# A Griffin-style layer in split fp32 on one core: the loads of the start untied from each other, and more units of the K loop done by Strassen products

## The chip, the core and the metric

The kernel runs on one core of one Trainium2 chip. A core has TensorE (PE, matrix products into PSUM), VectorE (DVE) and ScalarE (ACT) for elementwise work, GpSimd (POOL) for a few small operations and for issuing some transfers, and SyncE (SP), which here only issues transfers. Each engine takes its own instructions in order and waits on semaphores. The metric is the device time of one execution in microseconds.

## The reference

One layer on a residual stream x of 512 tokens by 2048 channels, all in float32 (cut; `GELU`, norms and attention are as they read):

```python
h = rmsnorm(x, attn_norm_g);  proj = h @ w_in                  # 2048 x 9216
u, v_sgu, q, k, v_att, g_a, g_b = split(proj)
y_a = chunked_spatial_gating(gelu(u), rmsnorm(gelu(v_sgu)), w_s, b_s)
y_b = stick_breaking_attention(rmsnorm(q), rmsnorm(k), v_att)
merged = sigmoid(g_a) * (y_a @ w_up_a) + sigmoid(g_b) * (y_b @ w_up_b)
x = x + merged @ w_o                                            # 2048 x 2048
hid = rmsnorm(x) @ w_ffn_in                                     # 2048 x 11264
x = x + (silu(gate) * up) @ w_ffn_out                           # 5632 x 2048
x = x + sigmoid(rmsnorm(x) @ w_ple_gate) * (p @ w_ple)
```

## The kernel before, in words

Everything is kept transposed, channels on the 128 partitions and the 512 tokens along the free axis. A float32 product is made of three matmuls: each operand is split into a high part (ACT copies it to fp32r: `whi` for weights, `parts` for activations) and a low part (DVE subtracts: `wlo`), and `mm3` adds hi*hi, hi*lo and lo*hi into PSUM (lines 268, 269 and 270).

The work is cut into **units**: 256 input channels by 256 output channels by 512 tokens. A *P* unit does the four 128x128 blocks plainly: 12 matmuls, 512 wide. An *S* unit does them as a Strassen form with seven products of blocks with 256 columns: 21 matmuls, 256 wide. Its activations need seven operand blocks (`Form`: the four blocks and three sums, all split), its weights too (`Weights`: two transfers from SP and one accumulating transfer from POOL into the same landing, two DVE sums, two ACT and two DVE splits). `Pair` works through all units of one output tile (256 channels); S units collect in banks that DVE and ACT mix at the end (line 673), P units add straight into y and z. Strings such as `OUT = "SSSSPPPP"` say which units of the K loop of a product are S and which P. The first output tile of every such product is done plainly. In w_in and w_ffn_in all units are S, for the most part in a doubled form (line 659, mixed at lines 702 and 705).

The stages follow each other: the first three products (`w_first`, eight K steps k with three P units each, while the x tiles are loaded, scaled, summed for the norm and split), the rest of w_in with attention and gating woven in, w_up_a/w_up_b, w_o, five small products of `w_ple`, w_ffn_in (44 tiles), w_ffn_out in three passes over K, and the gate w_ple_gate. Between stages the operand forms of the next product are made ahead, as room in two SBUF arenas (`parts` for split forms, `wholes` for raw blocks) comes free: `builds` is their queue, `tick` is called once or twice a unit and takes the next piece of such work.

Order: a scheduler that orders instructions by need sets each engine's order, except where extra edges hold it. `in_turn` keeps the weight splits and mixes in program order. `in_order` ties three kinds of loads on SP to one another: the first transfer of each weight block, and the x loads. `load_x` is called two steps ahead (`min(k + 3, KU)`).

A late S form (`late_form`, `plain_first`) makes its four sums (line 512, DVE) and then splits (lines 263 on ACT, 264 on DVE), when its turn in `builds` comes. `Norm.steps` (lines 907 to 933) sums squares over partitions with small matmuls (L914), makes diagonal matrices on DVE (L888) and multiplies them with ones on PE (L930), one piece a tick.

## Time and profile before

| | us |
|---|---|
| median of 3 runs | 2719.37 (2715.48 to 2728.74) |
| the profiled execution | 2723.71 |
| its span, first to last instruction | 2721.8 |
| PE busy | 2670.8 (98%) |
| DVE busy | 2166.5 (80%) |
| ACT busy | 1357.0 (50%) |
| POOL busy | 392.8 (14%) |

A busy PE is not a PE at its peak: matmuls overlap, so what a matmul costs is the distance from its start to the next one's start. The mean granted TensorE clock is 0.995. The stages stand at about 0 to 110 us (start), 110 to 860 (w_in), 860 to 1024 (w_up), 1024 to 1190 (w_o), 1190 to 1215 (w_ple), 1215 to 2064 (w_ffn_in), 2064 to 2246, 2246 to 2410 and 2410 to 2547 (the three passes of w_ffn_out) and from there the gate.

### The profile page before, as it was taken

Reading aid. Unit: us, or ns where it says so; the run is one execution under the profiler, and the core shown is the slowest. Engines: PE = TensorE matmul, PEld = TensorE weight load, DVE = VectorE, ACT = ScalarE, POOL = GpSimd, SP = SyncE. Lnnn points to the kernel's source line nnn. Section 1 sums busy time; section 2 is a strip of 40 time slices with the busy share of each in tenths; the row PEclk is TensorE's granted clock in tenths of the full one; section 3 lists DMA queues with packets and bytes.
Section 4 is the critical chain, followed back from the end, with each engine's and each line's share of the span. In section 5 each row is a group of like instructions: output and inputs, shape, how many; then the busy total and the mean of one; then the engine's idle time right before and its main releaser. Section 6 shows DMA issues by size and latency. Waiting matters only on the chain.

```text
span 2721.8 us, 43177 instructions
## 1 busy us (share of the span) xinstructions
PE 2670.8 (98%) x15907; PEld 2358.2 (87%) x15907; DVE 2166.5 (80%) x3715; ACT 1357.0 (50%) x2143; POOL 392.8 (14%) x439
## 2 busy tenths in 40 slices
PE   6999999999999999999999999999999999999999
PEld 5888888888888889988888888888888998989898
DVE  6687878788888657678989898989899567688876
ACT  6565656564555334365444444444445344454543
POOL 0112121211220000001111111111110111101110
PEclk8999999999999999999999999999999999999999
DMA  5667677777776447667888888788886668788784
GB/s 175 165 169 181 177 178 178 175 182 193 175 182 220 135 137 223 196 200 188 209 221 201 208 197 207 200 204 202 203 203 194 171 175 247 203 250 233 253 223 135
DMA packets 303412, 528.88 MB, mean 194 GB/s; under 512 B 25696, under 2 KB 162912, under 8 KB 303200
## 3 DMA queue, kind: packets, MB, share of 16 engines
q1 hardware_dynamic: 242448, 425.70, 49.1%
q0 software_dynamic: 60752, 100.43, 23.1%
q8 instruction: 125, 2.05, 0.3%
q14 instruction: 87, 0.71, 0.1%
HBM read 478.84 MB, written 47.19 MB: 193 GB/s over the span
## 4 chain that ended last, share of the span: by engine, by line
PE 84%; DVE 6%; DMA 4%; ACT 3%; issue 2%; POOL 0%; SPq 0%; DVEq 0%; ACTq 0%; POOLq 0%
PE ps L659 38%; PE ps L268 13%; PE ps L270 13%; PE ps L269 13%; PE small L659 4%; DVE wlo L344 2%; ACT whi L347 1%; DMA wholes<-w_in 1%; DVE parts L264 1%; DVE wholes L512 1%; DVE out L705 1%; DVE wholes L705 1%; PE small L1090 1%; PE small L1048 1%; DVE wholes L363 1%
## 5 line engine op out<-in xcount | busy, mean ns | idle before, releaser
L347 ACT ACTIVATE whi<-wholes 128x512 fp32r<-128x512 f32 (+4 forms) x950 | 846.9, 916 | 845.2 <-DVE wholes L363 286.4
L659 PE MATMUL ps<-parts,whi 128*128 128x512 f32 x3384 | 1127.1, 397 | 3.0 <-DVE p L705 1.9
L344 DVE TENSOR_TENSOR wlo<-wholes,whi 128x512 fp32r<-128x512 f32 (+4 forms) x950 | 961.6, 1044 | 97.5 <-ACT whi L347 96.5
L268 PE MATMUL ps<-parts,whi 128*128 128x256 f32 (+1 forms) x2675 | 857.3, 323 | 28.6 <-ACT whi L347 23.1
L269 PE MATMUL ps<-parts,whi 128*128 128x256 f32 (+1 forms) x2640 | 856.3, 324 | 0.9 <-DVE parts L264 0.9
L270 PE MATMUL ps<-parts,wlo 128*128 128x256 f32 (+1 forms) x2640 | 854.9, 324 | 1.8 <-DVE wlo L344 1.8
L659 PEld LDWEIGHTS ps<-parts,wlo 128*128 128x128 f32 x3384 | 634.9, 188 | 141.0
L659 PE MATMUL ps<-parts,wlo 128*128 128x256 f32 x3384 | 667.5, 278 | 0.0
L268 PEld LDWEIGHTS ps<-parts,whi 128*128 128x128 f32 x2675 | 509.5, 191 | 75.0 <-ACT whi L347 25.2
L659 PEld LDWEIGHTS ps<-parts,whi 128*128 128x128 f32 x3384 | 542.7, 189 | 10.2 <-issue 3.9
L269 PEld LDWEIGHTS ps<-parts,whi 128*128 128x128 f32 x2640 | 502.9, 191 | 45.1 <-DVE parts L264 2.2
L270 PEld LDWEIGHTS ps<-parts,wlo 128*128 128x128 f32 x2640 | 502.8, 190 | 41.0 <-DVE wlo L344 2.4
L363 DVE TENSOR_TENSOR wholes<-wholes 128x256 f32<-128x256 f32 (+1 forms) x794 | 327.7, 413 | 21.1 <-DMA wholes<-w_ffn_out 3.0
L351 POOL DMA_DIRECT2D wholes<-w_ffn_in x172 | 149.7, 870 | 752.4 <-DVE wlo L344 219.2
L705 DVE TENSOR_TENSOR out<-out,ps 128x256 f32<-128x256 f32 x373 | 152.9, 420 | 127.4 <-ACT out L702 116.6
L351 POOL DMA_DIRECT2D wholes<-w_in x132 | 116.7, 884 | 637.9 <-DMA wholes<-w_in 294.2
L264 DVE TENSOR_TENSOR parts<-wholes,parts 128x1024 fp32r<-128x1024 f32 (+3 forms) x129 | 122.4, 962 | 19.1 <-ACT parts L263 18.9
L659 PE MATMUL small<-parts,whi 128*128 128x512 f32 x344 | 136.0, 395 | 0.0
L1359 ACT ACTIVATE out<-out 128x512 f32<-128x512 f32 x44 | 27.8, 632 | 195.2 <-DVE out L1358 195.2
L263 ACT ACTIVATE parts<-wholes 128x1024 fp32r<-128x1024 f32 (+3 forms) x129 | 105.8, 844 | 32.7 <-DMA wholes<-hid 11.1
L351 POOL DMA_DIRECT2D wholes<-w_ffn_out x56 | 56.9, 1015 | 397.9 <-DMA wholes<-w_ffn_out 146.4
L673 DVE TENSOR_TENSOR out<-out 128x256 f32<-128x256 f32 x36 | 15.3, 424 | 120.5 <-ACT out L670 120.5
(125 smaller groups left out, 1655.2 us busy)
## 6 DMA issues: line engine op xcount, KB each, us to landing
wholes<-w_ffn_in SPq DMA_DIRECT2D x172, 384.0 KB, 5.5
wholes<-w_in SPq DMA_DIRECT2D x132, 384.0 KB, 5.1
wholes<-w_ffn_in SPq DMA_DIRECT2D x172, 256.0 KB, 4.7
wholes<-w_ffn_in POOLq DMA_DIRECT2D x172, 256.0 KB, 5.2
wholes<-w_in SPq DMA_DIRECT2D x132, 256.0 KB, 4.1
wholes<-w_in POOLq DMA_DIRECT2D x132, 256.0 KB, 4.9
wholes<-x SPq DMA_DIRECT2D x32, 512.0 KB, 5.4
wholes<-w_ffn_out SPq DMA_DIRECT2D x31, 512.0 KB, 4.2
```

The lines of the kernel that those rows point to most:

```text
L263: return (nc.scalar.activation(hi, src, AF.Copy), nc.vector.tensor_tensor(out=lo, in0=src, in1=hi.bitcast(F32), op=ALU.subtract))
L264: nc.vector.tensor_tensor(out=lo, in0=src, in1=hi.bitcast(F32), op=ALU.subtract))
L268: nc.tensor.matmul(ps[:, s], sh, mh[:, s], start=start, stop=False)
L269: nc.tensor.matmul(ps, sh, ml, start=False, stop=False)
L270: return nc.tensor.matmul(ps, sl, mh, start=False, stop=stop)
L344: in_turn(nc.vector.tensor_tensor(out=self.lo[:, blocks], in0=r, in1=h.bitcast(F32), op=ALU.subtract))
L347: in_turn(nc.scalar.activation(h, r, AF.Copy))
L351: nc.gpsimd.dma_start(out=raw[:, 3:5], in_=self.src[:, 1:3], accum_op=ALU.add)
L363: in_turn(nc.vector.tensor_tensor(out=o, in0=x, in1=y, op=ALU.add))
L659: i = nc.tensor.matmul(out, w, t, start=first and k == 0, stop=last and k == 1)
L705: in_turn(nc.vector.tensor_tensor(out=out, in0=x, in1=y, op=op))
L1359: nc.scalar.activation(g, g, AF.Silu)
```

## The change

Units: w_o has six S of eight in place of four, the first pass and the gate six of eight in place of five, the second pass six of seven in place of five. Since the first tile of the second product on is plain, that turns 16 + 7 + 7 + 7 = 37 P units into S units, one of them in the last tile of the gate. The last two S forms of w_o are made in the late form, with sums of their own.

Loads: `in_order` is gone, x loads are called when their step begins and take the block that was freed longest ago, p is loaded and split in halves, the first three results of w_ple are stored through POOL's queue, and five matmuls on zeros stand ahead of everything (`WARM`). In w_o the residual x is loaded three ticks into a tile, not a tile ahead, and the last tile is added to x before the second w_ple product, not after it.

Sums: `sum_early` scales a late form and makes its sums ahead of its turn, ten ticks after its fetch (`LANDS`), for the first three forms of the queue where room is. The norm's second matmul comes two ticks later.

The core of the diff:

```diff
-OUT = "SSSSPPPP"
-PASSES = "SSSSSPPP", "SSSSSPP", "SSSPPPP"
-GATE = "SSSSSPPP"
+OUT = "SSSSSSPP"
+PASSES = "SSSSSSPP", "SSSSSSP", "SSSPPPP"
+GATE = "SSSSSSPP"
+SUMMED = 4
+WARM = 5
+LANDS = 10
 def tick():
             if f.fetches and f.early and f.ready():
-                if fits([(wholes, f.fetches, "low"), (wholes, 1024, "low")]):
+                if fits([(wholes, f.fetches, "low")] + spare_blocks()):
                     f.fetch()
                 break
+        any(f.sum_early() for f in list(builds)[:FETCHED])
 class Weights:
             if kind == "P":
-                in_order(nc.sync.dma_start(out=raw, in_=src))
+                nc.sync.dma_start(out=raw, in_=src)
             else:
-                in_order(nc.sync.dma_start(out=raw[:, 3:5],
-                                           in_=src[:, 0:1].to_broadcast([P, 2, n * P])))
+                nc.sync.dma_start(out=raw[:, 3:5],
+                                  in_=src[:, 0:1].to_broadcast([P, 2, n * P]))
 class Form(Staged):
+        def sum_early(self):
+            if not self.late or self.sums or self.since is None or clock[0] < self.since + LANDS:
+                return False
+            if self.gain:
+                self.scale()
+            elif fits(SUMS + spare_blocks()):
+                self.sums = sums_of(self.raw)
+            return True
 def ple_operands():
-        raw = load(pT)
+        raw = take(1024)
         hi, lo = parts.take(1024, "high"), parts.take(1024, "high")
-        split_into(hi.own(), lo.own(), raw.f())
+        for s in (slice(0, T), slice(T, 2 * T)):
+            nc.sync.dma_start(out=raw.f()[:, s], in_=pT[:, s])
+            split_into(hi.own()[:, s], lo.own()[:, s], raw.f()[:, s])
 def ple_pair(j, planned=True):
-        nc.sync.dma_start(out=d, in_=o)
+        (nc.sync if planned else nc.gpsimd).dma_start(out=d, in_=o)
 def load_x():
-        x_raw.append(take(1024))
-        in_order(nc.sync.dma_start(out=x_raw[-1].f(), in_=xT[len(x_raw) - 1]))
+        x_raw.append(take(1024, "rested" if len(x_raw) < KU - 4 else "low"))
+        nc.sync.dma_start(out=x_raw[-1].f(), in_=xT[len(x_raw) - 1])
+    idle, nothing = wide(), bank()
+    nc.vector.memset(idle[:, : T // 2], 0.0)
+    for _ in range(WARM):
+        nc.tensor.matmul(nothing[:, :T // 2], idle[:, :P], idle[:, :T // 2],
+                         start=True, stop=True)
     ple_operands()
 class Norm: def steps
             diags = diagonals(self.cols)
             yield
+            yield
+            yield
 def x_form(k):
-            while len(x_raw) < min(k + 3, KU):
+            while len(x_raw) < min(k + 1, KU):
                 load_x()
+    def merged_form(j, kind):
+        src, ready = lambda: merged[j], lambda: j in merged
+        if kind == "S" and j >= SUMMED:
+            f = late_form(src, ready)
+            f.fetches, f.used = 0, True
+            return f
+        return form(kind, src, ready, raw=0, **({} if kind == "S" else {"how": "high"}))
@@ the w_o stage
-    raw = deque([load(xT[0])])
+    raw = deque()
     for j in range(KU):
-        if j < KU - 1:
-            raw.append(load(xT[j + 1]))
+        after(3, lambda j=j: raw.append(load(xT[j])))
         pr = pair(ms, last=j == KU - 1)
         if j == KU - 1:
             ple_pair(3)
-            ple_pair(4)
         h = raw.popleft()
         pr.onto(h.f())
+        if j == KU - 1:
+            ple_pair(4)
```

Three places in the engines' order. Lines of the changed kernel have other numbers: 859 is the old 830, 346 the old 347, 517 the old 499, 272 the old 263, 935 the old 901, 876 the old 847, 326 the old 327, 861 the old 832, 343/273/531/732 the old 344/264/512/705.

**SP at the start, before:** (L327 are weight blocks, L847 x tiles, L832 stores of w_ple results)

```order
L327 DMA wholes<-w_ple 128x512 x2
L327 DMA wholes<-w_first 128x512
L847 DMA wholes<-xT 128x1024
L832 DMA ple_107<-out_88 128x1024
L847 DMA wholes<-xT 128x1024
L832 DMA ple_158<-out_141 128x1024
L832 DMA ple_180<-out_163 128x1024
L847 DMA wholes<-xT 128x1024 x2
L327 DMA wholes<-w_first 128x512 x3
```

**and in the changed kernel:**

```order
L326 DMA wholes<-w_ple 128x512 x2
L326 DMA wholes<-w_first 128x512
L876 DMA wholes<-xT 128x1024 x2
L326 DMA wholes<-w_first 128x512 x5
L328 DMA wholes<-w_in 128x2x256
L326 DMA wholes<-w_first 128x512
L328 DMA wholes<-w_in 128x2x256
L326 DMA wholes<-w_first 128x512
L876 DMA wholes<-xT 128x1024
```

The second block of w_first stood behind three stores and five x loads on SP; now it stands behind three x loads and no store.

**ACT at the start, before:** (L830 evacuate w_ple results, L499 scale an x tile, L263 split it, L901 square it, L347 split a weight block; the last row here is the second block of w_first)

```order
L263 ACTIVATE parts<-wholes 128x4x256
L499 ACTIVATE wholes<-wholes,gcol 128x512
L901 ACTIVATE out_189<-wholes 128x1024
L499 ACTIVATE wholes<-wholes,gcol 128x512
L263 ACTIVATE parts<-wholes 128x4x256
L901 ACTIVATE out_215<-wholes 128x1024
L901 ACTIVATE out_228<-wholes 128x1024
L499 ACTIVATE wholes<-wholes,gcol 128x512 x2
L901 ACTIVATE out_292<-wholes 128x1024
L263 ACTIVATE parts<-wholes 128x4x256
L901 ACTIVATE out_354<-wholes 128x1024
L347 ACTIVATE whi_78<-wholes 128x512
```

**and in the changed kernel:** (`whi_78`, `whi_80` and `whi_76` are the second, third and fourth block of w_first)

```order
L859 ACTIVATE out_174<-ps_175 128x512
L346 ACTIVATE whi_78<-wholes 128x512
L859 ACTIVATE out_174<-ps_183 128x512
L517 ACTIVATE wholes<-wholes,gcol 128x512
L346 ACTIVATE whi_80<-wholes 128x512
L272 ACTIVATE parts<-wholes 128x4x256
L517 ACTIVATE wholes<-wholes,gcol 128x512
L935 ACTIVATE out_198<-wholes 128x1024
L517 ACTIVATE wholes<-wholes,gcol 128x512
L935 ACTIVATE out_224<-wholes 128x1024
L935 ACTIVATE out_237<-wholes 128x1024
L346 ACTIVATE whi_76<-wholes 128x512
```

The second block's split stood behind the squares of five x tiles (all five L901 rows); now no square stands ahead of it, and three stand between the third and the fourth block. Ahead of these rows the changed kernel has the split of the first block, two scalings, one small copy, one x split and two evacuations.

**DVE where w_ffn_in ends and the first pass begins, before:** (L512 and L264 make the pass's forms, L705 mixes w_ffn_in's last tile and so frees its banks)

```order
L512 TENSOR_TENSOR wholes<-wholes 128x256 x3
L264 TENSOR_TENSOR parts<-wholes,parts 128x4x256
L512 TENSOR_TENSOR wholes<-wholes 128x256 x4
L264 TENSOR_TENSOR parts<-wholes,parts 128x4x256
L512 TENSOR_TENSOR wholes<-wholes 128x256
L264 TENSOR_TENSOR parts<-wholes,parts 128x3x256
L512 TENSOR_TENSOR wholes<-wholes 128x256 x2
L264 TENSOR_TENSOR parts<-wholes,parts 128x4x256
L512 TENSOR_TENSOR wholes<-wholes 128x256
L264 TENSOR_TENSOR parts<-wholes,parts 128x3x256
L512 TENSOR_TENSOR wholes<-wholes 128x256
L705 TENSOR_TENSOR out_18698<-out_18698,ps_18567 128x256
```

**and in the changed kernel:**

```order
L273 TENSOR_TENSOR parts<-wholes,parts 128x4x256 x2
L273 TENSOR_TENSOR parts<-wholes,parts 128x3x256 x2
L531 TENSOR_TENSOR wholes<-wholes 128x256 x3
L273 TENSOR_TENSOR parts<-wholes,parts 128x4x256
L531 TENSOR_TENSOR wholes<-wholes 128x256
L732 TENSOR_TENSOR out_18921<-out_18921,ps_18796 128x256
```

Of twelve sums ahead of the first mix four are left; the five splits are the same.

More of the change, by code (lines that the diff above doesn't have):

```diff
@@ L220, in tick, with spare_blocks @@
                     reason="in its place among the units")
+    spared = [1]
+    def spare_blocks():
+        return [(wholes, 1024, "low")] * spared[0]
     class Staged:
@@ L290, in hybrid_layer @@
     chain = {}
-    def in_order(i):
-        if i.ins.engine in chain:
-            tc.add_manual_dep(
-                i.ins, chain[i.ins.engine],
-                mybir.DependencyInfo(mybir.DependencyClass.NoSync,
-                                     mybir.DependencyReason.DATA),
-                reason="in its place among the loads")
-        chain[i.ins.engine] = i.ins.name
     def in_turn(*instructions):
@@ L442, in __init__ @@
             self.src, self.fetches, self.raw, self.early = src, raw, None, False
+            self.late, self.gain, self.sums, self.since = False, None, None, None
         @property
         def sizes(self):
-            return self.places + [(wholes, self.fetches, "low")] * bool(self.fetches)
+            return (self.places + [(wholes, self.fetches, "low")] * bool(self.fetches)
+                    + SUMS * (self.late and self.sums is None))
         def fetch(self, block=None):
@@ L501, in gained, with sums_of @@
                 for i in range(2)]
-    def plain_first(form, raw):
-        b, s, v = cut(raw.f()), take(768, "tight"), take(256, "tight")
-        t, x = cut(s.f()), form.operand()
+    SUMS = [(wholes, 768, "tight"), (wholes, 256, "tight")]
+    def sums_of(raw):
+        b, s, v = cut(raw.f()), *(take(n, how) for _, n, how in SUMS)
+        t = cut(s.f())
         for out, p, q, op in ((t[:, 0], b[:, 1], b[:, 0], ALU.subtract),
@@ L512, in plain_first @@
             nc.vector.tensor_tensor(out=out, in0=p, in1=q, op=op)
+        return s, v
+    def plain_first(form, raw):
+        s, v = form.sums or sums_of(raw)
+        b, t, x = cut(raw.f()), cut(s.f()), form.operand()
         split_into(x[:, 0:4, 0], x[:, 0:4, 1], b)
@@ L530, in steps @@
             form.blocks = (parts.take(2 * PLACE, "place"),)
-            if gain:
-                gained(w.f(), w.f(), *gain)
-            yield
+            if not form.sums:
+                form.scale()
+                yield
             yield from plain_first(form, w)
             return form.operand()
-        return Form("S", steps, [(parts, 2 * PLACE, "place"), (wholes, 768, "tight"),
-                                 (wholes, 256, "tight")], ready, src, 1024)
+        f = Form("S", steps, [(parts, 2 * PLACE, "place")], ready, src, 1024)
+        f.late, f.gain = True, gain
+        return f
     def strassen_form(src, ready=always, gain=None, raw=PLACE):
@@ L1275, in hybrid_layer @@
     part, merged = {}, {}
-    ms = [form(k, lambda j=j: merged[j], lambda j=j: j in merged, raw=0, **how)
-          for j, k in enumerate(OUT) for how in [{} if k == "S" else {"how": "high"}]]
+    def merged_form(j, kind):
[3 more added lines that the diff above has]
+            f.fetches, f.used = 0, True
+            return f
+        return form(kind, src, ready, raw=0, **({} if kind == "S" else {"how": "high"}))
+    ms = [merged_form(j, k) for j, k in enumerate(OUT)]
     builds.extend(ms)
@@ L1280, in hybrid_layer @@
         for b in "ab":
-            s = load(gate_spill[b, j], PLACE if b == "b" and OUT[j] == "S" else 1024)
+            s = load(gate_spill[b, j], PLACE if b == "b" and j < SUMMED else 1024)
             g = s.f(0, 1024)
@@ L1388, in fetch @@
                     got[n] = load(spill[n, j])
+                if "x1" in names and j == KU - 1:
+                    spared[0] = 0
             if c:
```

9 lines of the change are left out of this document (8 added, 1 removed).

## The prediction, made before the result was known

> **What bounds the kernel now.** I began with the profile's header and its busy times.
>
> ```profile
> span 2721.8 us, 43177 instructions
> PE 2670.8 (98%) x15907; PEld 2358.2 (87%) x15907; DVE 2166.5 (80%) x3715; ACT 1357.0 (50%) x2143; POOL 392.8 (14%) x439
> ```
>
> PE is the bound: what it issues counts in full, and beside that only the moments when it stands. Where those are is in the busy times by stage (columns: window, its length, busy time and count of PE, PEld, DVE, ACT, POOL, then granted clock, DMA share, GB/s) and in PE's list of waits (total, times, longest).
>
> ```profile
> 0.00:35.00 35.00, 14.89 (x50) 10.82 (x51) 19.31 (x36) 22.38 (x32) 0.95 (x7) 0.84 0.56 191
> 1024.00:1190.00 166.00, 166.00 (x1046) 150.90 (x1046) 115.60 (x164) 75.42 (x89) 11.38 (x13) 1.00 0.64 187
> 1234.00:2064.00 830.00, 830.00 (x4766) 724.16 (x4766) 747.90 (x1353) 393.88 (x556) 145.24 (x167) 1.00 0.81 203
> 2262.00:2410.00 148.00, 146.25 (x996) 135.74 (x995) 110.22 (x184) 66.49 (x92) 20.10 (x20) 1.00 0.83 234
> ...
> PE ps L268 <- ACT whi L347: 23.1, 6, 12.9
> PE ps L268 <- ACT out L830: 2.8, 2, 1.5
> PE small L914 <- DVE wholes L905: 1.3, 1, 1.3
> ```
>
> In w_o and w_ffn_in PE never stands. Of 35 us at the start it stands 20, once for 12.9; the other waits of PE sit for the most part at the seams between stages. So the change has three places to gain: fewer PE cycles, the start, the seams.
>
> **The units.** Prices are distances between starts in the timeline of PE in the first tiles of the second pass (start, length, instruction):
>
> ```profile
> 2301.58 0.39 PE L268 MATMUL ps<-parts,whi 128*128 128x512 f32 x1
> 2303.62 0.39 PE L268 MATMUL ps<-parts,whi 128*128 128x512 f32 x1
> ...
> 2304.53 0.28 PE L270 MATMUL ps<-parts,wlo 128*128 128x256 f32 x1
> 2313.41 0.28 PE L269 MATMUL ps<-parts,whi 128*128 128x256 f32 x1
> ```
>
> Nine 512-wide matmuls take 2.04, so one takes 0.227; 74 of 256 take 8.88, so 0.120. A P unit is 12 x 0.227 = 2.72, an S unit 21 x 0.120 = 2.52: 0.20 saved. Thirty-six units outside the last tile give **-7.2**. The 37th is in the last gate tile, where the end is a chain on DVE:
>
> ```profile
> 2711.84 0.69 DVE L1428 TENSOR_TENSOR out<-ps,out 128x512 f32<-128x512 f32 x1 [2.65 <-PE ps L270]
> 2718.18 0.42 DVE L1441 TENSOR_TENSOR out<-out,wholes 128x256 f32<-128x256 f32 x1
> ```
>
> From y's end to the last DVE result are 6.8 us. With two P units in place of three y takes 12 matmuls, not 18, but one more S unit stands before it: 2.52 - 6 x 0.227 = 1.2 later. Behind it DVE has four operations of 0.69 and eight of 0.42 to do, 6.1, and I give it 6.3: **+0.6** in all. Together **-6.6** (-6 to -7.4).
>
> On other engines an S unit costs more than a P unit: more DVE work, an accumulating transfer, seven operand blocks for four. DVE has 50 of 166 us free in w_o; that is the cover, and what it fails to cover is below.
>
> **The start.** Timelines of PE, ACT and SP, and the clock of that window (columns there: length, PE busy, granted clock, DMA share, GB/s):
>
> ```profile
> 17.73 0.39 PE L268 MATMUL ps<-parts,whi 128*128 128x512 f32 x1
> 20.76 0.39 PE L270 MATMUL ps<-parts,wlo 128*128 128x512 f32 x1
> 34.06 0.79 PE L268 MATMUL ps<-parts,whi 128*128 128x512 f32 x1 [12.91 <-ACT whi L347]
> ...
> 13.60 0.63 ACT L347 ACTIVATE whi<-wholes 128x512 fp32r<-128x512 f32 x1 [1.03 <-DMA wholes<-w_ple]
> 19.13 0.60 ACT L830 ACTIVATE out<-ps 128x512 f32<-128x512 f32 x1
> 19.61 1.07 ACT L263 ACTIVATE parts<-wholes 128x1024 fp32r<-128x1024 f32 x1
> 20.55 0.73 ACT L499 ACTIVATE wholes<-wholes,gcol 128x512 f32<-128x512 f32 x1
> 21.17 1.06 ACT L901 ACTIVATE out<-wholes 128x1024 f32<-128x1024 f32 x1
> 29.00 1.33 ACT L499 ACTIVATE wholes<-wholes,gcol 128x512 f32<-128x512 f32 x2 [3.18 <-DMA wholes<-xT]
> ...
> 25.55 3.51 SPq L847 DMA_DIRECT2D wholes<-xT  x2
> 29.12 1.37 SPq L327 DMA_DIRECT2D wholes<-w_first  x3
> ...
> 24.00:37.70 13.70, 3.64 (x9) 0.50 0.68 219
> ```
>
> The first unit of w_first begins at 17.73 and ends at 21.0. The second waits until 34.06 for its high part, because SP issues x tiles first and ACT stands on an x tile before it comes to the weights. The clock then falls to 0.50 and PE works its first 3.6 us (34.06 to 37.7) at half speed. So the gap costs 13.1 (34.06 - 20.76 - 0.23) and the clock 1.8.
>
> In the changed order, counted on ACT from the first block's split (13.60 before): two scalings 1.5, a small copy 0.3, an x split 1.07, three evacuations 1.8, then the second block's split 0.6: 5.2, so it is ready at 18.8, or at 17.3 since p and x come sooner. PE needs it 2.72 after the first unit's start, at 20.4 or 18.9. The gap goes. But the squares stand between the third and fourth block: to the fourth 0.6 + 0.73 + 0.6 + 1.07 + 0.73 + 1.06 + 0.73 + 2.1 + 0.6 = 8.2, so 25.5 to 27, against PE's need at 24.1 to 25.9, 1.3 late. The squares also need output buffers that the stores of w_ple hold, now on POOL's queue. The nearest rows (microseconds to landing, last) are
>
> ```profile
> ple<-out SPq DMA_DIRECT2D x8, 512.0 KB, 5.2
> wholes<-w_o POOLq DMA_DIRECT2D x16, 256.0 KB, 5.8
> ```
>
> so some 6 from issue; that adds 1 to 2. I price the new wait at 3, half a microsecond is won ahead of it (p in halves), and the five matmuls on zeros at nothing: 13.1 + 1.8 + 0.5 - 3 = **-12.5**. Bounds: -4 (three such waits with the clock halved after each) and -17 (none). From there on DVE has some 62 us of work (7.7 a step) beside 65 of PE, so no more is gained.
>
> **The seams.** Each seam costs twice: PE stands, and the clock halves behind it.
>
> ```profile
> 1225.54 0.39 PE L270 MATMUL ps<-parts,wlo 128*128 128x512 f32 x1
> 1228.23 1.04 PE L930 MATMUL small<-out,ones 128*128 128x128 f32 x6 [2.30 <-DVE out L888]
> 1228.90:1232.30 3.40, 3.40 (x12) 0.50 0.60 112
> ...
> 2075.62 0.77 PE L268 MATMUL ps<-parts,whi 128*128 128x512 f32 x1 [2.40 <-DVE out L705]
> 2075.40:2078.80 3.40, 3.17 (x8) 0.51 0.49 158
> 2556.70:2560.10 3.40, 3.40 (x10) 0.50 0.99 336
> ```
>
> After 2.30, 2.40 and (the L914 row above) 1.3 us of standing the clock is 0.50 for 3.4 us, which loses 1.7.
>
> The Trainium skill (TensorE: Matmul & The Clock Gate, "HAM oscillation — how this bites in real kernels") has it that only gaps beyond about 3.4 us halve the clock. These rows disagree, and the measurement decides; by the page the two seams below would return 3.4 less.
>
> *Second norm:* the matmul on the diagonals (L930) comes 23 rows of 512-wide matmuls later on PE, 5.2 us, more than the 2.3 it waited: **-4.1** (0 to -4.2). Late next is the row it makes, which w_ffn_in's first tile needs on DVE; a tile of 19 us covers that.
>
> *w_ple:* the two waits for L830 (2.8 in all) are evacuations that find no free output buffer; the last w_o tile now gives its buffer back before the second product: **-2.5** (0 to -2.8).
>
> *First pass:* PE waits 2.40 for the mix L705, which on DVE stands behind twelve sums. Eight are made earlier:
>
> ```profile
> 2065.89 1.09 DVE L512 TENSOR_TENSOR wholes<-wholes 128x256 f32<-128x256 f32 x3
> 2074.73 0.42 DVE L512 TENSOR_TENSOR wholes<-wholes 128x256 f32<-128x256 f32 x1
> 2075.07 1.07 DVE L705 TENSOR_TENSOR out<-out,ps 128x256 f32<-128x256 f32 x3
> ```
>
> Three take 1.09, so eight 2.9: the wait and its half clock go, **-4** (0 to -4.1). The sums themselves go to w_ffn_in, where DVE has 82 of 830 us free.
>
> *Other seams* (second and third pass, gate): fewer late sums, but one more S form each; the gate's norm matmul stands five matmuls, 1.1 us, later, nearly its whole wait of 1.3. **-1.5** (+3 to -5).
>
> *New:* w_o's first tile needs two more S forms.
>
> ```profile
> 1005.00:1024.00 19.00, 19.00 (x96) 16.19 (x95) 17.83 (x21) 12.27 (x12) 0.94 (x2) 1.00 0.65 180
> 1024.00:1045.00 21.00, 21.00 (x135) 19.12 (x135) 16.17 (x22) 9.29 (x11) 2.13 (x3) 1.00 0.78 246
> ```
>
> Each is four sums and splits of 1024, 768 and 256 in place of one of 1024, about 3 us more, and a third double of S weights adds 1.8: 8 us for 6 that DVE has free. **+2** (0 to +5).
>
> **Sum.** -12.5 - 6.6 - 4.1 - 2.5 - 4 - 1.5 + 2 = -29.2. The profiled span of 2721.8 becomes 2692.6; that execution took 2723.71, 1.9 more, so 2694.5; it was 4.3 above the median of 2719.37. On the median the forecast is **2690**, 1.1% less.
>
> **Rivals.**
>
> *The start only moves its wait.* ACT stands on the stores through POOL, on x tiles called one step ahead rather than three, and DVE at 7.7 of 8.2 us a step never makes up for it. For: ACT's and DVE's in-order queues, which made the old gap. Against: the second and third block no longer stand behind them. Start -4 in place of -12.5: 2699.
>
> *The seams hold.* The extra S forms put back on DVE what early sums take off, and the three seam terms (10.6) stay. For: the first-pass term has only half a microsecond to spare. Against: norm and w_ple are cured by order, not by DVE time. 2701. With the start's rival together, 2709.
>
> *More is gained.* No new wait at the start, the gate's clock stays up: 2690 - 4.5 - 4 - 2 - 2 = 2677.
>
> *The clock's fall is not tied to short gaps.* Then only the standing time returns at the two seams: 2690 + 3.4 = 2693. (The page named above gives this; against it stand the three rows of 0.50.)
>
> *Slower: the weight chain of S doubles.* A third double of S weights in each tile of w_o, first pass and gate takes the place of a P double: 3.0 us of DVE for 1.2, three transfers for one, the last through POOL (5.8 to landing, above) and behind the other two. It decides where it makes PE stand over 29 / 29 = 1.0 us in each of the 8 + 7 + 7 + 7 tiles; at 1.6 the time is 2690 + 46 = 2736. For: DMA share is already 0.83 in the second pass. Against: w_ffn_in has nothing but S doubles, faster ones, and PE busy 830 of 830.
>
> That the change doesn't do what it says I give nothing: the changed program has 438 fewer 512-wide and 765 more 256-wide matmuls.
>
> **How the numbers follow.** Forecast 0.58, start 0.15, seams 0.12, both 0.05, more 0.05, the clock's rival 0.02, slower 0.03. The forecast's own spread is some 10 us; 2675 to 2707 holds it and the rivals of one kind. Less than 0.5% (13.6 us, about what this kernel's runs can tell from none) is a change that ends between 2706 and 2733: both rivals together and tails of the single ones, 0.09. Faster 0.88, slower 0.03.
>
> **What would show it.** In the profile after: the first 35 us with PE busy some 25 and the clock above 0.5 in 24 to 38; L930's successor gone from PE's waits, L705's too; clock 1.00 where w_ffn_in begins and ends; w_o tiles 0.4 us shorter, the first and third product of w_ffn_out likewise by their count of changed units. Wrong it would be if PE stood for `whi` several times before 90 us, for `parts` at the beginning of w_o, or in every tile for S weights.

## The result

The changed kernel took 2701.22 us (median of 4 runs, 2694.93 to 2702.91) where the kernel before took 2721.74 (median of 4, 2715.48 to 2728.74). The ratio is 0.9913, with a 95% interval of 0.9895 to 0.9931: 0.87% faster, 20.5 us. In a second set, of five runs beside the kernel before, it was 0.993 (0.9916 to 0.9943). The forecast was 2690, 1.1% less; the measured time lies inside the stated range of 2675 to 2707.

So sign and size are about right. The terms of the sum are not. They are compared here in the profiled executions, which took 2723.71 before and 2700.52 after, with these headers and rows of busy time after:

```profile
span 2698.7 us, 43910 instructions
PE 2664.3 (99%) x16244; PEld 2369.2 (88%) x16244; DVE 2201.6 (82%) x3750; ACT 1368.7 (51%) x2143; POOL 388.7 (14%) x450
```

The stretches are bounded by starts of matmuls in PE's timeline: the first of a w_in head, and the last in the doubled S form (L659, in the changed kernel L686) of w_in and of w_ffn_in.

| stretch | before, us | after, us | difference | forecast |
|---|---|---|---|---|
| start to the first matmul of a w_in head | 113.9 | 96.2 | -17.7 | -12.5 |
| w_in to its last tile | 731.6 | 735.4 | +3.7 | 0 |
| w_up, w_o, w_ple, w_ffn_in | 1227.3 | 1222.9 | -4.4 | -7.8 |
| w_ffn_out, gate, end | 649.0 | 644.3 | -4.7 | -8.9 |
| span | 2721.8 | 2698.7 | -23.1 | -29.2 |

The start gave 5 us more than forecast, w_in took back 3.7 that nothing in the forecast spoke of, and the seams gave almost nothing. The busy times of stretches in the changed kernel (columns as in the prediction: window, length, PE, PEld, DVE, ACT, POOL, granted clock, DMA share, GB/s) show the start, w_o, the first tile of w_ffn_out, and between them three stretches of 3.4 us:

```profile
0.00:35.00 35.00, 30.75 (x120) 23.61 (x121) 22.54 (x44) 27.21 (x43) 4.59 (x12) 1.00 0.80 256
125.00:128.40 3.40, 3.20 (x14) 3.21 (x15) 2.70 (x10) 2.94 (x7) 0.91 (x1) 0.50 0.65 122
1007.30:1168.40 161.10, 161.10 (x1192) 154.13 (x1191) 124.90 (x182) 79.28 (x96) 17.36 (x20) 1.00 0.76 212
1210.40:1213.80 3.40, 3.40 (x12) 2.84 (x12) 3.40 (x4) 1.98 (x4) 0.87 (x1) 0.50 0.72 136
2054.30:2073.90 19.60, 16.87 (x78) 13.53 (x77) 19.46 (x38) 11.24 (x14) 1.74 (x2) 1.00 0.73 193
2073.90:2077.30 3.40, 3.40 (x10) 2.62 (x9) 3.40 (x5) 0.00 (x0) 0.00 (x0) 0.51 0.87 274
2535.30:2538.70 3.40, 3.14 (x18) 2.76 (x19) 3.06 (x7) 2.63 (x4) 0.00 (x0) 1.00 0.77 275
```

The first 35 us hold 30.75 us of PE where they held 14.89; 4.5 of them are the matmuls on zeros. In w_o PE is busy for every microsecond, as before. But the second norm (1210) and the first pass (2074) are still followed by a half clock, and w_in (125) has a new one; only at the gate (2535) has it gone. PE's list of waits in the changed kernel says what stands there now (total, times, longest):

```profile
PE ps L277 <- ACT whi L346: 4.1, 6, 1.3
PE ps L277 <- ACT parts L272: 3.1, 2, 2.1
PE ps L278 <- DVE parts L273: 2.9, 2, 2.0
PE small L1114 <- DVE sp L273: 2.5, 1, 2.5
PE ps L277 <- ACT out L859: 1.4, 1, 1.4
PE small L948 <- DVE wholes L939: 1.3, 1, 1.3
```

The waits for `whi` fell from 23.1 to 4.1: the gap of 12.9 is gone, with no other of its size. The wait for the second norm's diagonals and the one for the mix are gone too, as the forecast's signs asked. In their places stand a wait for ACT's split of an activation block (L272, 2.1 at the second norm) and one for DVE's (L273, 2.0 in the first pass). Both are new, and the experiments are about them, the start, and the new wait in w_in (L1114).

### The profile page after: what moved, and what is told of

Same layout as the page of the kernel before. It is cut to its first block, busy times and chain, and to the rows that moved or that the text cites. A ratio compares the mean times of both kernels' runs of the same rounds, so it can differ in the third digit from the quotient of the medians.

```text
span 2698.7 us, 43910 instructions
## 1 busy us (share of the span) xinstructions
PE 2664.3 (99%) x16244; PEld 2369.2 (88%) x16244; DVE 2201.6 (82%) x3750; ACT 1368.7 (51%) x2143; POOL 388.7 (14%) x450
## 3 DMA queue, kind: packets, MB, share of 16 engines
q8 instruction: 127, 2.08, 0.3%
## 4 chain that ended last, share of the span: by engine, by line
PE 82%; DVE 9%; DMA 3%; ACT 3%; issue 2%; POOL 1%; SPq 0%; DVEq 0%; ACTq 0%; POOLq 0%
PE ps L686 37%; PE ps L279 13%; PE ps L277 13%; PE ps L278 13%; PE small L686 4%; DVE wlo L343 3%; DVE out L732 1%; DVE parts L273 1%; ACT whi L346 1%; DMA wholes<-w_in 1%; DVE wholes L531 1%; DVE wholes L732 1%; DMA wholes<-x 1%; PE small L1126 1%; PE small L1084 1%
## 5 line engine op out<-in xcount | busy, mean ns | idle before, releaser
L346 ACT ACTIVATE whi<-wholes 128x512 fp32r<-128x512 f32 (+3 forms) x937 | 854.9, 938 | 834.2 <-PE ps L278 318.3
L686 PE MATMUL ps<-parts,whi 128*128 128x512 f32 x3384 | 1129.3, 398 | 4.2 <-DVE p L732 2.9
L343 DVE TENSOR_TENSOR wlo<-wholes,whi 128x512 fp32r<-128x512 f32 (+3 forms) x937 | 972.8, 1072 | 63.6 <-ACT whi L346 61.6
L277 PE MATMUL ps<-parts,whi 128*128 128x256 f32 (+1 forms) x2784 | 869.5, 315 | 8.9 <-ACT whi L346 4.1
L278 PE MATMUL ps<-parts,whi 128*128 128x256 f32 (+1 forms) x2749 | 869.5, 317 | 2.9 <-DVE parts L273 2.9
L279 PE MATMUL ps<-parts,wlo 128*128 128x256 f32 (+1 forms) x2749 | 867.4, 317 | 1.7 <-DVE wlo L343 1.7
L686 PEld LDWEIGHTS ps<-parts,wlo 128*128 128x128 f32 x3384 | 635.8, 188 | 142.3 <-DVE wlo L343 1.2
L686 PE MATMUL ps<-parts,wlo 128*128 128x256 f32 x3384 | 668.3, 279 | 0.8 <-DVE wlo L343 0.8
L277 PEld LDWEIGHTS ps<-parts,whi 128*128 128x128 f32 x2784 | 529.7, 190 | 49.4 <-ACT whi L346 7.1
L278 PEld LDWEIGHTS ps<-parts,whi 128*128 128x128 f32 x2749 | 523.3, 190 | 40.3 <-DVE parts L273 3.5
L279 PEld LDWEIGHTS ps<-parts,wlo 128*128 128x128 f32 x2749 | 523.3, 190 | 35.5 <-DVE wlo L343 3.0
L686 PEld LDWEIGHTS ps<-parts,whi 128*128 128x128 f32 x3384 | 543.8, 189 | 12.1 <-DVE p L732 4.4
L362 DVE TENSOR_TENSOR wholes<-wholes 128x256 f32<-128x256 f32 (+1 forms) x810 | 339.6, 419 | 35.4 <-issue 11.8
L273 DVE TENSOR_TENSOR parts<-wholes,parts 128x1024 fp32r<-128x1024 f32 (+4 forms) x142 | 130.3, 932 | 10.2 <-ACT parts L272 10.0
L686 PE MATMUL small<-parts,whi 128*128 128x512 f32 x344 | 136.0, 395 | 0.0
L272 ACT ACTIVATE parts<-wholes 128x1024 fp32r<-128x1024 f32 (+4 forms) x142 | 111.8, 821 | 34.8 <-DMA wholes<-hid 13.5
L350 POOL DMA_DIRECT2D wholes<-w_ffn_out x56 | 50.9, 908 | 403.3 <-DMA wholes<-w_ffn_out 119.5
```

The lines of the kernel that those rows point to most:

```text
L272: return (nc.scalar.activation(hi, src, AF.Copy), nc.vector.tensor_tensor(out=lo, in0=src, in1=hi.bitcast(F32), op=ALU.subtract))
L273: nc.vector.tensor_tensor(out=lo, in0=src, in1=hi.bitcast(F32), op=ALU.subtract))
L277: nc.tensor.matmul(ps[:, s], sh, mh[:, s], start=start, stop=False)
L278: nc.tensor.matmul(ps, sh, ml, start=False, stop=False)
L279: return nc.tensor.matmul(ps, sl, mh, start=False, stop=stop)
L343: in_turn(nc.vector.tensor_tensor(out=self.lo[:, blocks], in0=r, in1=h.bitcast(F32), op=ALU.subtract))
```

## Experiments

Unless another kernel is named, an edit starts from the changed kernel. Where one run is named, the time is that of a single profiled execution, and the runs of the changed kernel alone spread over 9 us; most readings below are therefore of a place in the trace, where repeated runs of one program differ by 0.1 to 1 us.

### Fewer Strassen units

```diff
-OUT = "SSSSSSPP"
-PASSES = "SSSSSSPP", "SSSSSSP", "SSSPPPP"
-GATE = "SSSSSSPP"
+OUT = "SSSSPPPP"
+PASSES = "SSSSSPPP", "SSSSSPP", "SSSPPPP"
+GATE = "SSSSSPPP"
```

> The changed kernel with the unit strings of before (four of eight Strassen units in w_o, five, five and three in the passes, five in the gate); loads, early sums and order stay changed. Two theories of why the first pass still opens with waits (0.9 for the high half of a weight, 2.15 for the parts of a block, then 3.4 us at half clock) although the mix is no longer late. A, the S forms: the sixth S unit has put four sums and a second split (some 3 us of DVE) into the first tile, where DVE has no idle time left. Then with five S units these two waits together fall below 1 us, the clock stays at 1.00 there, and the work that PE issues grows by 3.2 (w_o, 16 units of 0.20), 2.8 (passes) and 2.6 (gate, of which 1 is given back behind it): about 8 - 1 - 3 - 1.7 = +2 us, 2703. B, late transfers: the blocks of hid and the weights land late whatever the forms are. Then both waits stay near 3 us with the half clock, and the time is +7.6, 2709. Both expect tiles of w_o of 21.0 us instead of 20.6.

2704.92 us (4 runs, 2704.25 to 2708.97), ratio 0.9935 (0.9912 to 0.9958): nearer to theory A's 2703 than to B's 2709. PE's waits in the first pass:

```profile
2068.04 0.39 PE L277 MATMUL ps<-parts,whi 128*128 128x256 f32 x1 [0.73 <-ACT whi L346]
2069.32 0.50 PE L278 MATMUL ps<-parts,whi 128*128 128x512 f32 x1 [0.19 <-DVE parts L273]
```

The wait for DVE's parts is 0.19 with five S units and 1.99 with six, and the half clock behind it is gone. So at the first pass it is the sixth S form that makes PE stand. The second pass, which also has a unit fewer here, opens with a wait of 2.17 and a half clock instead, so part of what was saved was lost again there. PE does not stand at the second norm either: the last read of x1, which is late in the changed kernel (below), goes out at 1190.3 here, 5.7 us after the store of that block, where the changed kernel has 1198.6, 16.7 after it; and the stretch from w_up to w_ffn_in is only 0.7 longer, although its 16 units cost 3.2. So the 37 units, priced at 6.6, are worth 3.7 by the medians (the intervals of the ratios overlap): part of what they save PE comes back as waits at these two seams.

### No early sums

```diff
 def sum_early(self):
-    if not self.late or self.sums or self.since is None or clock[0] < self.since + LANDS:
-        return False
+    if True:
+        return False
```

> The changed kernel without early sums: every sum of a late S form is made in the first tile again, so the first pass makes 24 sums there, not 16. A, DVE bounds that tile: eight sums are 2.9 us more on DVE there, so the waits of PE in the first 20 us of the first pass rise from 3.05 to about 6 us, of which one may again be for the mix of the last tile before; the whole kernel +3, 2704. B, transfers bound that tile: the waits stay within 0.5 us of 3.05, the whole kernel is unchanged.

The same edit was run again later on top of two others (below), where PE's clock did not fall in the middle of the place. There PE's waits around the beginning of the first pass were:

```profile
2058.22 0.47 PE L277 MATMUL ps<-parts,whi 128*128 128x512 f32 x1 [2.40 <-DVE out L732]
2070.58 0.39 PE L277 MATMUL ps<-parts,whi 128*128 128x256 f32 x1 [0.73 <-ACT whi L346]
2076.40 0.50 PE L278 MATMUL ps<-parts,whi 128*128 128x512 f32 x1 [1.98 <-DVE parts L273]
```

The wait for the mix is back with the 2.40 us of the kernel before, and the waits behind it are unchanged: 5.1 of standing where the changed kernel has 2.7. That is theory A. In the first of the two runs (2705.32) the clock was 0.5 for 3.4 us behind the mix, so that PE came to its blocks 1.7 us later, and the wait for `parts` shrank to 0.36: a delay of PE gave DVE time. Both show the same thing. In these 20 us DVE is the bound (19.46 of 19.60 us busy, in the row above), and PE stands for whatever DVE is late with.

### Nothing ahead of the first product

```diff
-WARM = 5
+WARM = 0
```

> The changed kernel without the five matmuls on zeros ahead of the first product. A, the zeros set the clock: the clock is 0.50 from the start to about 10.4 us as in the kernel before, PE's 512-wide matmuls come 0.43 apart until then, and w_in begins about 1.5 to 2 us later (16 matmuls at 0.2 more each from 6.1 us on, less 0.7 because the first product starts at 6.1 and not at 6.8). B, they do nothing: clock 1.00 from the first product on, and w_in begins 0 to 0.7 us earlier than at 96.2. My prediction gave them no price, so by it B.

2702.2 (one run); w_in began at 98.3. PE's timeline at the beginning, and the row of its clock:

```profile
6.08 0.80 PE L277 MATMUL ps<-parts,whi 128*128 128x512 f32 x1 [6.08 <-ACT whi L346]
7.10 0.63 PE L279 MATMUL ps<-parts,wlo 128*128 128x512 f32 x1
7.53 0.63 PE L277 MATMUL ps<-parts,whi 128*128 128x512 f32 x1
```

```profile
6.00:10.40 4.40, 4.32 (x10) 3.41 (x11) 2.16 (x5) 2.46 (x6) 0.00 (x0) 1.00 0.99 351
```

The matmuls come 0.43 apart until 10.5, half the rate of the 0.23 that they reach after that; with the zeros they come 0.23 apart from the second one on. So A in its mechanism. Ten matmuls lose 0.2 each, 2.0, and the first product began 0.7 earlier without the zeros: an estimate from these is that they are worth about 1.3. In time that is not to be told from the spread, since six profiles with the zeros and otherwise the same start began w_in at 96.0 to 98.3, at 97.0 in the mean. The clock's row reads 1.00 all the while, not 0.50 as expected, and so it does in the kernel before, whose matmuls come 0.43 apart up to 10.4: before the first change of the clock in these traces the row does not tell the rate; the distance between matmuls does. The Trainium skill (TensorE: Matmul & The Clock Gate, "Part 1: The HAM clock gate") puts the doubling of the rate some 4 us into sustained matmuls, give or take half a microsecond; the 4.4 us here agree.

### The last block of x1 stays

```diff
 def keep_for(form, block, j):
-    if (j < KU - KEPT or form.raw or late and late[0] is not form
-            or not fits([(wholes, 1024, "low")] * 2)):
+    if (j < KU - KEPT or form.raw or late and late[0] is not form and j < KU - 1
+            or not fits([(wholes, 1024, "low")] * (2 if j < KU - 1 else 1))):
```

In the changed kernel the seam between w_ple and w_ffn_in reads as follows (SP's, ACT's and PE's timelines in turn): the read of x1's last block is issued, its first reader waits for it to land, then splits it after the high half of a weight, and PE starts.

```profile
1198.62 0.49 SPq L513 DMA_DIRECT2D wholes<-x  x1
...
1206.65 1.34 ACT L517 ACTIVATE wholes<-wholes,gcol 128x512 f32<-128x512 f32 x2 [2.59 <-DMA wholes<-x]
1207.90 1.25 ACT L346 ACTIVATE whi<-wholes 128x1280 fp32r<-128x1280 f32 x1
1209.06 1.04 ACT L272 ACTIVATE parts<-wholes 128x1024 fp32r<-128x1024 f32 x1
...
1210.15 1.00 PE L277 MATMUL ps<-parts,whi 128*128 128x512 f32 x2 [2.08 <-ACT parts L272]
```

> The changed kernel, but the last block of x1 stays in the on-chip memory for its S form instead of being stored and read back (the read was issued at 1198.6 and landed at 1206.6; the scaling, the split and then PE waited for it: 2.08 us at 1208, and 3.4 us at half clock behind it). A, the seam's new wait is that transfer: wait and half clock go, -2.2 - 1.7 = -3.9 us, 2697; w_ffn_in begins at clock 1.00. B, the wait only passes to the next thing (the read of the block before it, which goes out later now, or the row of the norm that the first tile needs on DVE): a wait of 1.5 to 2.5 us with its half clock stands within 10 us of the same place, and the time is unchanged, 2701.

2693.41 us (4 runs, 2691.51 to 2693.74), ratio 0.9890 (0.9863 to 0.9917), the lowest time of all. PE does not stand at the seam at all, and the clock stays at 1.00, as its row shows:

```profile
1190.00:1215.00 25.00, 25.00 (x126) 21.21 (x125) 23.56 (x45) 20.92 (x33) 5.96 (x6) 1.00 0.96 269
```

That is theory A. It gained more than was expected, about 8 us beside the changed kernel. In the profiles the stretch from w_up to w_ffn_in became 4.3 shorter, w_in 2.4 (no half clock there this time), and w_ffn_out 3.4, in which the waits of 0.9 to 1.0 at the heads of the second and third pass are gone: the arena's places fall otherwise, and in DVE's order twelve sums, four each of the second pass's, the third's and the gate's forms, now stand earlier. That these sums are what took the waits away was not tried apart.

### The start: the tie between loads, and the x tiles

The first kernel restores both parts (the tie for w_first's loads, shown, and likewise for x's and the doubles'), the second only the number of x tiles called ahead.

```diff
+                in_order(nc.sync.dma_start(out=raw, in_=src))
...
-            while len(x_raw) < min(k + 1, KU):
+            while len(x_raw) < min(k + 3, KU):
```

> The changed kernel with two parts of the start undone: x tiles are called three steps ahead of their use, and the loads on SP's queue are tied to the order in which they are written, as before. The halves of p, the results of w_ple stored through POOL and the zeros stay changed. A, the old gap came from the order of the loads (x tiles ahead of the weights on SP, and ACT standing on x): a wait of PE for the high half of a weight of 8 to 13 us comes back between 17 and 35 us, with its half clock, and w_in begins 8 to 15 us later than at 96.2 to 97.4. B, the gap went because of the other parts (operands of p sooner, stores off SP): the longest wait before 40 us stays under 3 us and w_in begins within 2 us of 97.

2720.31 (one run), with w_in at 107.8: nearly all of the gain is lost. SP's timeline, then PE's waits between 17 and 36:

```profile
4.56 17.96 SPq L886 DMA_DIRECT2D wholes<-xT  x4
22.56 1.38 SPq L336 DMA_DIRECT2D wholes<-w_first  x3
...
27.46 0.79 PE L277 MATMUL ps<-parts,whi 128*128 128x512 f32 x1 [8.45 <-ACT whi L356]
```

18 us pass on SP until four x tiles are out, and the weights that PE needs stand behind them. The gap and its half clock are back: A. They are not all of the loss: w_in begins 11.6 later than in the changed kernel's profile, and then takes 5.6 longer, with two half clocks in it.

> The changed kernel with only the first of these two undone: x tiles are called three steps ahead, the tie between the loads stays away, so that on SP five loads of w_first follow the fourth x tile instead of the third. A, it is the tie that makes SP hold the weights back, not the number of x tiles called: w_in begins within 1.5 us of 97. B, each x tile called early takes a place of the on-chip memory and 512 KB of transfers from the weights: waits for the high half of a weight grow by 2 to 6 us before 40 us and w_in begins at 99 to 103.

2697.25 (one run), w_in at 94.5: A again, and 1.7 us sooner than in the changed kernel's profile. Calling the tiles early does not hold the weights back by itself; with the tie it does. The tie without the early calls was not run. The whole time lies inside the spread of the changed kernel.

### The norm's two steps

```diff
             diags = diagonals(self.cols)
             yield
-            yield
-            yield
```

> The changed kernel without the two extra steps between the diagonals and their matmul in the norms, so that the matmul of the second norm stands where it stood before, behind the second block's rows. A, the seam is bound by the read of the last block of x1, and the place of the norm's matmul only decides where PE stands for it: a wait of 2 to 2.5 us for the diagonals comes back at the second norm, the wait for the split of x1 (2.08) goes or falls below 0.7 us, and the stretch from w_in's end to w_ffn_in's end changes by less than 1.5 us. B, both waits stand one behind the other: that stretch grows by 2 to 4 us. In the first norm (at 80 to 90 us) two waits of 0.5 to 2 us may come back by either.

2704.61 (one run). PE's wait at the second norm:

```profile
1212.21 1.75 PE L964 MATMUL small<-out,ones 128*128 128x128 f32 x6 [3.96 <-DVE out L922]
```

It stands 3.96 for the diagonals, longer than expected, and no longer for the split; the stretch from w_up to w_ffn_in is 1.2 us longer than with the two steps. That is A. The steps move PE's standing from one thing that waits for x1 to another and save about 1 us. At the first norm no wait came back.

### w_in's first head

In the changed kernel POOL, DVE and PE read, in their timelines around 122:

```profile
122.83 0.86 POOL L350 DMA_DIRECT2D wholes<-w_in  x1 [4.91 <-ACT wholes L1091]
123.39 1.36 POOL L1036 TENSOR_TENSOR rr<-ms,expo 128x4 f32<-128x4 f32 x1
...
124.78 0.17 DVE L1052 TENSOR_SCALAR rr<-rr 128x4 f32<-128x4 f32 x1 [3.35 <-POOL rr L1036]
...
125.20 0.48 PE L1114 MATMUL small<-sp,tri 128*128 128x128 f32 x1 [2.45 <-DVE sp L273]
```

The power that makes rr stands behind an accumulating transfer on POOL, DVE's scaling waits for it, and the split of sp behind the scaling comes too late for PE.

```diff
             token_rms(ps, r)
+            yield 2
             nc.vector.tensor_scalar(out=r, in0=r, scalar1=float(P) ** -0.5, scalar2=None,
                                     op0=ALU.mult)
-            yield 2
```

> The changed kernel with one small operation of DVE moved in w_in: the scaling of the norm's row rr, which waits for a power on POOL, goes out two steps later, behind the split of sp. In the changed kernel PE waited 2.45 us there for that split (at 122), with 3.4 us at half clock behind it. A, the queue: the split itself has its data long before and only stands behind the scaling on DVE, the scaling behind the power on POOL, and the power behind an accumulating transfer of w_in that waits for an earlier one to land. Then the wait falls below 0.5 us and its half clock goes; in the later heads nothing changes by more than 0.5: w_in becomes 2.5 to 4 us shorter (735.4 to 731.5 to 733), the whole kernel 2697 to 2699. B, sp's own data are late (ACT's half of the split, or its source): the wait stays at 2.5 to 2.9 us.

2702.58 (4 runs), ratio 0.9919 (0.9901 to 0.9936), no different from the changed kernel. PE's wait there:

```profile
129.44 1.56 PE L1084 MATMUL small<-wholes 128*128 128x384 f32 x2 [2.58 <-ACT wholes L1041]
```

The wait for sp is gone, as A said, and its length is not: PE now stands for the next reader of rr, on ACT. So it is rr that is late. The kernel before has the same order on POOL, with a shorter wait:

```profile
141.04 0.33 PE L1078 MATMUL small<-sp,tri 128*128 128x128 f32 x1 [1.05 <-DVE sp L264]
```

Its transfer went out 0.6 us after rr's input was ready, in the changed kernel 2.0 after. Why the transfer goes out later was not settled. The profile names an operation of ACT (L1091) as what released it, where the expectation has an earlier transfer that must land.

### On one chip: again, and three kernels on top

The changed kernel was run once more. The second kernel keeps the last block of x1 and calls x tiles three steps ahead. The third is the second with five S units in the first pass in place of six, the fourth is the second without the early sums.

```diff
-PASSES = "SSSSSSPP", "SSSSSSP", "SSSPPPP"
+PASSES = "SSSSSPPP", "SSSSSSP", "SSSPPPP"      # in the third kernel
```

> The changed kernel once more, beside the next three on the same chip: 2698 to 2703, with the waits at the second norm (2.1 to 2.8), at the first pass (0.9 and 2.15) and in w_in's first head (2.4 to 2.9). If the halved clock behind a wait depends on the moment at which the wait falls, it follows some of these waits here and not the same ones as in the first profile; if it depends on the length of the wait alone, the same ones.

2701.53 (5 runs), ratio 0.993 (0.9916 to 0.9943). PE's waits are those of the first profile within 0.4 us. The clock behind them is not (rows behind w_in's head, the second norm, the first pass, the gate's norm):

```profile
125.60:129.00 3.40, 3.40 (x14) 3.21 (x15) 2.67 (x9) 2.95 (x7) 0.91 (x1) 0.50 0.71 120
1211.30:1214.70 3.40, 3.35 (x17) 2.91 (x18) 3.40 (x4) 1.86 (x4) 0.88 (x1) 1.00 0.82 156
2072.20:2075.60 3.40, 3.30 (x14) 2.73 (x15) 3.40 (x5) 0.85 (x1) 0.00 (x0) 1.00 0.95 319
2535.10:2538.50 3.40, 3.40 (x9) 2.61 (x10) 3.23 (x5) 1.76 (x3) 0.00 (x0) 0.54 1.03 356
```

> The changed kernel with the last block of x1 kept on the chip and x tiles called three steps ahead at the start. A, the two gains are independent (8 and 1.7 us in their own runs): 2690 to 2693. B, the earlier x tiles only made a lucky start: 2693 to 2695, with w_in beginning at 96 to 97.5 and not at 94.5.

2694.53 (4 runs, 2692.95 to 2697.58), ratio 0.9902 (0.9889 to 0.9916), 7 us under the changed kernel on the same chip, and no better than keeping the block alone. The time is B's, but its account is not: w_in does begin at 94.5, where keeping the block alone had 97.4, but then PE waits in w_in's first heads.

```profile
110.34 0.66 PE L1019 MATMUL small<-ident,out 128*128 128x128 f32 x4 [1.94 <-ACT sq L1026]
```

In the profiles w_in takes 6.1 longer than with the block alone; this wait, which neither run with one of the two edits alone has, and a half clock at 127 (1.7) are 3.6 of that. Why the wait appears was not tried.

> As the one before, with five Strassen units of eight in the first pass instead of six (7 or 8 units of 0.20 more for PE, 1.4 to 1.6). A, the wait of 2.15 for the parts of a block in the first pass comes from DVE, which makes the sixth S form there: the wait falls below 0.5, with the half clock that follows it in some executions, so w_ffn_out is 0.5 to 2.3 us shorter, 2689 to 2692. B, it comes from blocks of hid that land late: the wait stays and w_ffn_out is 1.5 longer, 2692 to 2695.

2696.65 (4 runs, 2692.16 to 2698.14), ratio 0.9906 (0.9892 to 0.992). PE's wait for the parts at the first pass is 0.18, so the sixth S form made it there: A. But the second pass then opens worse, with this row of PE:

```profile
2242.14 0.58 PE L279 MATMUL ps<-parts,wlo 128*128 128x256 f32 x1 [3.44 <-DVE wlo L343]
```

With a dearer unit and this wait, w_ffn_out came out 1.6 longer, not shorter. The wait was moved once more.

> As the second of these, without early sums. A, early sums are worth what moves off DVE's worst tile: the mix of the last tile of w_ffn_in waits again behind the sums (2.4 to 2.6 us) and the wait for the parts (2.15) goes, so at the first pass some 1 us is lost, and up to 3 at the second and third, 2692 to 2696. B, they are worth what I predicted, 4 us at the first pass: 2695 to 2698. C, they only move waits: within 1 us of the second of these.

2700.62 (5 runs, 2697.19 to 2704.38), ratio 0.9921 (0.9909 to 0.9934), 6 us over the kernel with the sums. The first pass loses 2.4 of standing (the rows under "No early sums"), and waits of 1.0, 1.0 and 1.4 open the second and third pass. A had the wait for the mix right, but the wait for the parts, which it expected to go, stayed at 1.98. The time is theory B's, but it is not the first pass alone that gives it.

## Why the prediction was right, and where it was not

**The start: -12.5 forecast, -17.7 measured.** The step that named the cause held: the order of the loads made the gap of 13.1 and the half clock of 1.8, and with the tie and the early x calls restored a wait of 8.45 came back. The new wait at the fourth block was there, at 23.7, for 1.3 us instead of 3. Three gains were left out. I priced the matmuls on zeros at nothing, and without them ten matmuls run at half rate (about 1.3). And the wait of 1.9 for a high half at 60 and those of 2.3 for the first norm's diagonals went as well, where I had said that no more was to be gained from DVE's 62 us of work beside PE's 65. Why these two went was not tried; the norm's two steps are not the reason, as no wait came back without them.

**w_in: nothing forecast, +3.7.** A wait of 2.45 in place of 1.05, and a half clock, are 3.1 of it. The forecast took a stage whose order is unchanged to take the same time, and no experiment changed only its beginning. In the other kernels the stage took 732 to 741, always longer than the 731.6 of before. That it meets other transfers still under way, because it begins 18 us sooner, was argued, not shown.

**The units: -6.6 forecast, -6.4 measured, before the waits.** A w_o tile took 20.61 instead of 21.01, two units of 0.20, 3.2 in all. The passes give 14 times 0.20 by count, 2.8; their whole stretch is 2.6 shorter. From the last P units of the third pass to the end 0.4 went besides the half clock, where I had 0.6. The price from distances between starts in the trace was exact. What it left out is what the forms of these units make PE wait for elsewhere: in whole time the run without them was 3.7 slower.

**New waits in w_o: +2 forecast, none.** PE was busy 161.10 of 161.10 us. DVE, which I gave 8 us more for 6 free ones, was busy 19.79 of 20.7 in the first tile. That was 3.6 more than before, and it just fitted.

**The second norm: -4.1 forecast, -0.2.** This step failed. I read that the diagonals would be ready in time and took the row that the norm makes for the next late thing. The next late thing was already in the trace of before, in part hidden behind the wait: the read of x1's last block (SP's and ACT's timelines).

```profile
1214.96 1.26 SPq L495 DMA_DIRECT2D wholes<-x  x1
1222.51 1.34 ACT L499 ACTIVATE wholes<-wholes,gcol 128x512 f32<-128x512 f32 x2 [2.45 <-DMA wholes<-x]
```

There the block's low half was ready at 1226.8, 0.8 after PE began to stand, and DVE made the diagonals behind it. In the changed kernel the read goes out 9.5 us ahead of PE's standing instead of 11.0, takes 0.5 longer to land, and the block's split stands behind a high half of 1.25. So with the matmul out of the way PE stood 2.08 for the block instead of 2.30 for the diagonals, with the same half clock behind it; in the second profile that one stayed away. Keeping the block on the chip took both away.

**w_ple: -2.5 forecast, -1.4.** One of the two waits for an evacuation is gone, one of 1.44 is left. No run was made on it, and in the other kernels it lay between 0.7 and 2.9, so its cause stays open.

**The first pass: -4 forecast, -0.4.** The early sums did what the step said: the mix is no longer late, and without them its wait of 2.40 is back. What was left out is the same change's sixth S form. Its four sums and second split, some 3 us, fall to DVE in that very tile. I had counted it for the other seams, in their bounds, and not here. With five units the wait for the parts is 0.19.

**Other seams: -1.5 forecast, -1.3.** Those of the second and third pass became 0.4 longer. The other 1.7, at the gate, is a half clock that did not follow there this time and did in the second profile, so it is no effect of the change.

So of the rivals "the seams hold" was nearest. Of the 10.6 us that it said would stay, all but about 2 stayed, and for the first pass by its mechanism, the S forms that fill DVE again. But the part of it that said order cures norm and w_ple was wrong for the norm. Its time, 2701, was met to the microsecond by accident: the start gave 5 more and w_in took 4 back. "The start only moves its wait" (2699) and the slower case, the chain of S doubles, fell: nothing in the trace stands for S weights tile by tile. The rival that the clock's fall is not tied to short gaps fell as well, though the step "a wait means a half clock behind it" is not right as I used it either, as the last section shows.

The terms on the path were wrong by up to 5 us each, and three of them, at the seams, leaned the same way, towards a wait that goes and leaves nothing behind. What brought the sum near was the start, the one place where the wait was so long that what is late next could not fill it. That errors of up to 5 us each added up to no more than 6 of 29 was luck.

## What to carry to other kernels

Before a wait is priced as gained, look at which input of the same stretch of work arrives next, and when. At the second norm here it could be found in the trace of before, hidden behind the first wait; at the first pass the change itself made it. At both, the new wait was within half a microsecond of the old one. When several parts of one change meet in one tile, add up the busiest engine of that tile once for all of them. A block that has just been made and is read back a few microseconds later is worth keeping: here that change of two lines gained 8 us, beside 20.5 of the whole change, though half of it in other places than the seam.

## What the runs showed of the hardware

**The half clock behind a short wait comes and goes.** The same matmul of the first pass waited 2.13 to 2.15 us beyond its normal distance in ten profiles of kernels with six S units; the clock was half for 3.4 us behind it in seven of them and stayed at 1.00 in three. The same program, run twice, had it behind the second norm and the first pass the one time, and behind the gate's norm the other, on waits equal within 0.1. Waits of 1.3 to 1.6 at the gate were followed by it in some profiles, one of 2.52 in w_in (the kernel that keeps x1's block) was not. So the length of a wait does not decide it alone.

The traces show what does. In each of the fourteen profiles all half-clock stretches begin on one grid of 3.413 us, to 0.01 us, and last one step of it or a whole number of steps (6.83, 10.24, 13.65), but for those that the end of the trace cuts off. What counts is how long PE stands within one step of the grid. Of the whole steps at full clock from 10.5 us on, 28 had more than 1.9 us of standing by PE's rows, and the clock was half in the step behind every one of them; of 82 with 1.0 to 1.9 it was behind twelve; of 151 with 0.6 to 1.0 behind none. The three waits in the first pass without a half clock lay across a border of the grid (0.86 and 1.11, 0.96 and 1.03, 0.73 and 1.26), and so did the one of 2.52 (0.92 and 1.60). The grid lies elsewhere in each run, so the same wait is whole within a step in one and cut in two in another. The Trainium skill (TensorE: Matmul & The Clock Gate, "Part 1: The HAM clock gate") says that PE's activity is judged over windows of some 3.4 us that run freely, whatever the kernel does; the grid of 3.413 agrees. It also says that the clock falls after an idle window of about that length, and here 1.9 us of standing within one were always enough; the measurement decides. Each such stretch of 3.4 us costs 1.7. Four places that may have it or not make up to 7, which is near the 8.0 between the fastest and the slowest run of the changed kernel; that this is what spreads them was argued, not shown.

**A delay of PE is time for the engine that it waits for.** In the first run without early sums 3.4 us at half clock cut the next wait from 1.98 to 0.36. A half clock ahead of a seam where DVE is the bound therefore costs less than its 1.7.
